# Feed forward part of a fused two-block kernel: eight raw slots in the second matrix product, another place for the residual loads and the additions, some sums of factors on GpSimd

## The chip, the cores and the metric

The kernel runs on one core of one Trainium2 chip. The metric is device time in microseconds of one execution, as the median over several runs. All work is in float32; a matrix product is made of three passes (see below), and the engines involved are TensorE (PE, with its weight loads PEld), VectorE (DVE), ScalarE (ACT), GpSimd (POOL) and SyncE, whose queue (SPq) issues every DMA of this kernel in one fixed order.

## The reference

Two model parts run one after the other: two layers of attention and mLSTM over 1024 tokens, and then a block of four mixers with an output projection, followed by the feed forward part that this change is in. The reference's feed forward, with `x` of 1024 tokens by 1024 channels:

```python
h = _rmsnorm(x, norm2_g)
u = h @ w_up            # 1024 x 4096
u = jnp.square(jax.nn.relu(u))
x = x + u @ w_down      # 4096 x 1024
return _rmsnorm(x, final_g)
```

## The kernel before

The feed forward is two large products, here called the up product (`up`, L2043) and the down product (`down`, L2105). Both use Strassen's scheme: each matrix is cut into 2x2 blocks, and seven products of sums of blocks (tables `UP` and `DOWN`) replace eight. For the down product a row of the table says which blocks of the hidden matrix are added or subtracted to make the left factor, which blocks of `w_down` make the right factor, and to which output blocks the result is added. Output block (t, n) is half t of the tokens and half n of the channels.

Each of the seven products is cut into eight units, j = 0 to 7. A unit is 24 matmuls of 128x128 by 128x512: every factor is split into a high and a low float32r half (`split`: a copy on ACT at L249 gives the high half, a subtraction on DVE at L250 gives the low half), and `mm3` (L244 to L246) multiplies high by high, high by low and low by high.

The data of a unit comes in as raw tiles of 128 x 1024 float32 (512 KB). In the up product these are weights only, one or two tiles per unit (L2034). In the down product they are weights (L2142) and those hidden blocks that were written to DRAM, tensor `hd` (L2134); the hidden blocks (1,0) and (1,1) stay on chip in 16 slots `H`. Per unit the seven down products load three, three, three, three, two, one and three raw tiles. All raw tiles go through one ring of six slots, two in the arena `fa` and four in the arena `t816a`; a load can only be issued when the slot's former owner has been read for the last time, that is after the sum (for the second tile of a sum) or after the low half at L250 (for the tile that holds the sum). When a factor is a sum of two blocks, DVE makes it (L2038 for up weights, L2022 for the left factors of the up product, L2119 in the down product).

The code makes the operands of a unit two units ahead of its matmuls. The results of a down product lie in four PSUM banks; the next product uses the other four. After each product DVE adds every bank to its output blocks in `x` (L2176, four or eight additions of 128x512). The rows of `x` in the first token half are complete after the fifth product, those of the second half after the seventh; then the final norm (`rms_row`: square on ACT at L469, three small steps on DVE and GpSimd, one scaling on DVE at L1382) and the store to `out` follow.

The order of the instructions on each engine is not the order of the code: the block is ordered by a scheduler that runs a timeline, and takes from each engine's waiting instructions by readiness and then by place in the code. Each engine then works through its own list in order, and an instruction that waits holds everything behind it on its engine.

Of the kernel before, what the change touches and what calls it, by code (L numbers as in the profile page):

```python
# [10 lines left out]
ALU = mybir.AluOpType  # L11
# [153 lines left out]
class Fill:  # L165
# [5 lines left out]
    def add(self, *gens):  # L171
        self.q.extend(gens)
# [9 lines left out]
    def finish(self):  # L182
        while self.q:
            self.step()
# [6 lines left out]
class Kernel:  # L191
# [1821 lines left out]
    def up_tokens(self, m):  # L2013

        blocks, op = self.UP[m][:2]
        h, l = self.rop.get([128, 4, 512]), self.rop.get([128, 4, 512])
        yield h, l
        for k in (0, 2):
            src = [self.z[:, 4 * c + k:4 * c + k + 2, t * 512:t * 512 + 512] for t, c in blocks]
            if op:  # L2020
                r = self.rtmp.get([128, 2, 512])
                self.nc.vector.tensor_tensor(r.ap, *src, op=op)  # L2022
                src = [r.ap]
            self.split(h[:, k:k + 2], l[:, k:k + 2], src[0])
            yield h, l

    def up_weights(self, m, j, raw):

        blocks, op = self.UP[m][2:4]
        rs = []  # L2030
        for k, n in blocks:
            r = raw.get([128, 4, 256])
            o = n * 2048 + j * 256
            self.nc.sync.dma_start(  # L2034
                r.ap, self.A["w_up_2"][0][k * 512:k * 512 + 512, o:o + 256].rearrange("(k p) c -> p k c", p=128))
            rs.append(r)
        if op:
            self.nc.vector.tensor_tensor(rs[0].ap, rs[0].ap, rs[1].ap, op=op)  # L2038
        h, l = self.rwh.get([128, 4, 256]), self.rwl.get([128, 4, 256])
        self.split(h.ap, l.ap, rs[0].ap)  # L2040
        return h, l

    def up(self, cur, raw, ahead):  # L2043

        nc, V = self.nc, self.nc.vector
# [10 lines left out]
        for i, (m, j) in enumerate(units):  # L2056
            if i + 2 < len(units):
                ahead.append(self.up_weights(*units[i + 2], raw))
            if j == 0:
                h, l = cur  # L2060
                nxt = self.up_tokens(m + 1) if m < 6 else None
            if nxt and j in (2, 3, 4):
                cur = next(nxt)
            w = ahead.pop(0)
            outs = [(c, sign, (c, j) not in acc) for c, sign in self.UP[m][4]]
            for c, _, first in outs:
# [38 lines left out]
    def down(self, raw):  # L2105
        nc, V, A = self.nc, self.nc.vector, self.A
        rw = Ring(self.xa, [4096 + 1024 * i for i in range(4)] + [1024 * i for i in range(4)], 1024)
        rx = self.F(0, 1024, 8)
        x = [rx.get() for t in range(8)]
        for t in range(8):  # L2110
            nc.sync.dma_start(x[t].ap, self.x4[t * 128:t * 128 + 128])
        fg = self.F(8192, 1024, 1).get()
        nc.sync.dma_start(fg.ap, A["final_g_2"].unsqueeze(0).broadcast_to([128, 1024]))
        self.rny = Ring(self.ta, [s[1] for s in self.cs.free_[:2]], 1024)

        def factor(rs, op, h, l):
            if op:
                r = rs[0][0] if rs[0][1] else rs[1][0] if rs[1][1] else raw.get([128, 2, 512])
                V.tensor_tensor(r.ap, rs[0][0].ap, rs[1][0].ap, op=op)  # L2119
            else:  # L2120
                r = rs[0][0]
            self.split(h.ap, l.ap, r.ap)

        def operands(m, j):
# [9 lines left out]
                    nc.sync.dma_start(r.ap, self.hd[f:f + 2].rearrange("f p t -> p f t"))  # L2134
                    rs.append((r, True))
            hid = self.rwh.get([128, 2, 512]), self.rwl.get([128, 2, 512])
            factor(rs, aop, *hid)
            rs = []
            for c, n in bb:
                r = raw.get([128, 2, 512])  # L2140
# [2 lines left out]
                    r.ap, A["w_down_2"][0][f:f + 256, n * 512:n * 512 + 512].rearrange("(f p) c -> p f c", p=128))  # L2143
                rs.append((r, True))
            w = rw.get([128, 2, 512]), rw.get([128, 2, 512])
            factor(rs, bop, *w)
            return hid, w

        def product(p, o, j, tt):
            (hh, hl), (wh, wl) = o  # L2150
            ts = slice(tt * 128, tt * 128 + 128)
            for i in range(2):
                self.mm3(p.ap, hh[:, i, ts], hl[:, i, ts], wh[:, i], wl[:, i], j + i == 0, j == 7 and i == 1)

        units = [(m, j) for m in range(7) for j in range(8)]
        ahead = [operands(*u) for u in units[:2]]
        todo = units[2:]
        for m in range(7):
            ps = [self.pg.get() for _ in range(4)]
            last = []  # L2160
            for j in range(8):
                if todo and not last:
                    ahead.append(operands(*todo.pop(0)))
                o = ahead.pop(0)
                if m == 6 and j >= 6:
                    last.append((j, o))
                    continue
                for tt in range(4):
                    product(ps[tt], o, j, tt)
                self.done([o[0]])  # L2170
            for tt in range(4):
                for j, o in last:
                    product(ps[tt], o, j, tt)
                for (t, n), sign in self.DOWN[m][4]:
                    y = x[4 * t + tt][:, n * 512:n * 512 + 512]
                    V.tensor_tensor(y, y, ps[tt].ap, op=ALU.add if sign > 0 else ALU.subtract)  # L2176
                if m in (4, 6):
                    t = 4 * (m == 6) + tt
                    self.rms_row(x[t].ap, fg.ap)
                    nc.sync.dma_start(A["out"][t * 128:t * 128 + 128], x[t].ap)  # L2180
        self.done([o[0] for _, o in last])

    def run(self):
# [49 lines left out]
```

## Time and profile before

| | |
|---|---|
| median of 3 runs | 2801.44 us (2795.85 to 2803.32) |
| profiled execution, its own time | 2799.03 us |
| its span, first to last instruction | 2797.3 us |
| PE busy | 2630.7 us (94%) |
| DVE busy | 1865.4 us (67%) |
| ACT busy | 1449.1 us (52%) |
| POOL busy | 481.5 us (17%) |
| mean granted TensorE clock | 0.979 of full speed |

The profiled execution is 2.4 us under the median of the runs. A matmul's record begins before the one in front of it has ended, so PE's busy time is not a measure of how full it is; the distance between the starts of matmuls is. The up product's matmuls begin at about 2141.0 us of the span, the down product's at about 2456.0, and the last matmul of all ends at 2789.4.

### The profile page before, as it was taken

The page shows a single profiled execution, that of the slowest core. Times are in us where ns is not written, and L with a number is a line of the kernel's source. Part 1 is how long each engine was busy: PE and PEld are TensorE (multiplying, and loading weights), DVE is VectorE, ACT ScalarE, POOL GpSimd, SP SyncE. Part 2 cuts the span into 40 slices and gives each one's busy share as a digit, 9 for nine tenths or more (in the row PEclk, how much of TensorE's full clock was granted, in tenths as well). Part 3 has the DMA queues.
Part 4 walks back from the last instruction along what each step waited for, and adds up shares of the span by engine and source line. Part 5 has one row for each costly group of instructions (what it writes and reads, how often), then busy time and mean ns, then how long its engine had stood idle before and what let it go on. Part 6 is the DMA issues. An engine that isn't in the chain of part 4 may idle for free. (4 is left out here: it accounts for less than half of the span.)

```text
span 2797.3 us, 43718 instructions
## 1 busy us (share of the span) xinstructions
PE 2630.7 (94%) x16222; PEld 2277.3 (81%) x16222; DVE 1865.4 (67%) x3750; ACT 1449.1 (52%) x3023; POOL 481.5 (17%) x686
## 2 busy tenths in 40 slices
PE   7999989999999999999998989898899999999998
PEld 3888878998889787978988878688798777877786
DVE  4788755536756788665365369977724586857886
ACT  4666545546624666555464153478715535643343
POOL 0122203414200122123132030144400000000000
PEclk9999999999999999999999989999899999999999
DMA  7001021212554101021124441422234667677855
GB/s 249 26 18 57 26 56 40 59 45 71 159 184 153 57 17 54 27 67 58 51 64 147 154 143 42 143 80 89 93 106 158 205 200 244 201 241 251 257 171 179
DMA packets 302241, 324.73 MB, mean 116 GB/s; under 512 B 17904, under 2 KB 242508, under 8 KB 301772
## 3 DMA queue, kind: packets, MB, share of 16 engines
q1 hardware_dynamic: 302028, 321.95, 36.5%
q8 instruction: 127, 2.08, 0.3%
q14 instruction: 86, 0.70, 0.1%
HBM read 274.86 MB, written 47.03 MB: 115 GB/s over the span
## 5 line engine op out<-in xcount | busy, mean ns | idle before, releaser
L246 PE MATMUL psum<-xa 128*128 128x512 f32 (+2 forms) x2136 | 751.4, 352 | 25.5 <-DVE xa L250 24.5
L244 PE MATMUL psum<-xa 128*128 128x512 f32 (+2 forms) x2136 | 757.5, 356 | 13.1 <-ACT xa L249 5.0
L245 PE MATMUL psum<-xa 128*128 128x512 f32 (+2 forms) x2136 | 751.2, 352 | 0.9 <-DVE xa L266 0.8
L246 PEld LDWEIGHTS psum<-xa 128*128 128x128 f32 x2136 | 408.8, 191 | 84.5 <-DVE xa L250 34.5
L244 PEld LDWEIGHTS psum<-xa 128*128 128x128 f32 x2136 | 409.9, 192 | 66.9 <-ACT xa L249 6.4
L245 PEld LDWEIGHTS psum<-xa 128*128 128x128 f32 x2136 | 409.1, 192 | 50.5 <-DVE xa L266 1.6
L464 POOL TENSOR_TENSOR rsb<-rsa,half 128x1 f32<-128x1 f32 (+1 forms) x129 | 93.9, 729 | 1088.1 <-DVE rsa L462 1017.1
L244 PE MATMUL psum<-xa,xg 128*128 128x256 f32 (+1 forms) x864 | 248.5, 288 | 1.9 <-DVE fa L1522 1.2
L245 PE MATMUL psum<-xa,xg 128*128 128x256 f32 (+1 forms) x864 | 246.1, 285 | 0.0
L246 PE MATMUL psum<-xa,xg 128*128 128x256 f32 (+1 forms) x864 | 245.8, 285 | 0.0
L249 ACT ACTIVATE xa<-t816a 128x1024 fp32r<-128x1024 f32 x125 | 131.0, 1056 | 206.6 <-DVE t816a L2119 110.9
L265 ACT ACTIVATE xa<-fa 128x1024 fp32r<-128x1024 f32 (+1 forms) x104 | 109.9, 1059 | 195.4 <-PE psum L246 110.5
L266 DVE TENSOR_TENSOR xa<-fa,xa 128x1024 fp32r<-128x1024 f32 (+1 forms) x94 | 115.3, 1229 | 133.6 <-ACT xa L265 123.1
L805 POOL TENSOR_SCALAR fa<-fa,esk 128x640 f32<-128x640 f32 (+2 forms) x144 | 112.1, 791 | 451.9 <-DVE esk L803 363.4
L244 PEld LDWEIGHTS psum<-xa,xg 128*128 128x128 f32 x864 | 164.0, 190 | 3.2 <-DVE fa L1522 1.6
L250 DVE TENSOR_TENSOR xa<-t816a,xa 128x1024 fp32r<-128x1024 f32 x125 | 151.3, 1219 | 21.2 <-ACT xa L249 13.1
L245 PEld LDWEIGHTS psum<-xa,xg 128*128 128x128 f32 x864 | 164.0, 190 | 0.8 <-issue 0.7
L246 PEld LDWEIGHTS psum<-xa,xg 128*128 128x128 f32 x864 | 163.7, 190 | 0.4 <-issue 0.3
L244 PE MATMUL psum<-xg,xa 128*128 128x512 f32 x376 | 153.2, 408 | 3.9 <-DVE fa L1764 2.8
L246 PE MATMUL psum<-xg,xa 128*128 128x512 f32 x376 | 151.7, 404 | 1.0 <-POOL xa L266 1.0
L245 PE MATMUL psum<-xg,xa 128*128 128x512 f32 x376 | 152.1, 404 | 0.2 <-DVE xg L250 0.2
L1008 DVE SCALAR_TENSOR_TENSOR fa<-fa,vec 128x640 f32<-128x640 f32 (+2 forms) x128 | 110.5, 869 | 51.7 <-ACT fa L1006 50.5
(500 smaller groups left out, 5870.4 us busy)
## 6 DMA issues: line engine op xcount, KB each, us to landing
fa<-in_w_in_dram SPq DMA_DIRECT2D x64, 512.0 KB
t816a<-in_w_up_dram SPq DMA_DIRECT2D x62, 512.0 KB
t816a<-in_w_down_dram SPq DMA_DIRECT2D x57, 512.0 KB
fa<-in_w_ada_dram SPq DMA_DIRECT2D x48, 512.0 KB
t816a<-hd SPq DMA_DIRECT2D x40, 512.0 KB
fa<-in_w_down_dram SPq DMA_DIRECT2D x39, 512.0 KB
fa<-in_w_up_dram SPq DMA_DIRECT2D x34, 512.0 KB
fa<-in_w_out_dram SPq DMA_DIRECT2D x24, 512.0 KB
```

The source lines that it names most:

```text
L244: mm(out, lh, rh, start=start, stop=False)
L245: mm(out, lh, rl, start=False, stop=False)
L246: mm(out, ll, rh, start=False, stop=stop)
L249: self.nc.scalar.activation(hi, src, AF.Copy)
L250: self.nc.vector.tensor_tensor(lo, src, hi.bitcast(F32), op=ALU.subtract)
L265: self.nc.scalar.activation(h.ap, r.ap, AF.Copy)
L266: (self.nc.gpsimd if self.wpool else self.nc.vector).tensor_tensor(l.ap, r.ap, h.ap.bitcast(F32), op=ALU.subtract)
L464: self.nc.gpsimd.tensor_tensor(r, e, self.half.broadcast_to([128, m]), op=ALU.pow)
L805: nc.gpsimd.tensor_scalar(P[j][:, :nk], P[j][:, :nk], e[:, j:j + 1], 0.0, op0=ALU.mult, op1=ALU.add)
L1008: nc.vector.scalar_tensor_tensor(y, U[i][:, lo + tap:hi + tap], col(tap), y, op0=ALU.mult, op1=ALU.add)
```

## The change

Five things change, in `up_tokens`, `up_weights`, `up` and `down`:

- In `down` the raw ring gets the two slots of the arena that are free by then, so it has eight; the two new ones are used first, and the scratch of the final norm moves to slots of hidden block (1,1).
- The loads of the residual `x` stand in `up` within the seventh product (L2069) and not at the head of `down` (L2111 before).
- In `down` the additions of a finished product are written one bank at a time between the units of the next product, and the final norm of the first token half is written within the seventh product, not after the fifth.
- In `down`, for products with a sum in both factors (the third, fourth and seventh), the left factor's sum of odd units goes to GpSimd: 12 sums.
- In `up`, the weight sum of odd units in the third product (4 sums) and both sums of the left factor of the fourth product (2 sums) go to GpSimd.

```diff
@@ up_tokens
-                self.nc.vector.tensor_tensor(r.ap, *src, op=op)
+                (self.nc.gpsimd if m == 3 else self.nc.vector).tensor_tensor(r.ap, *src, op=op)
@@ up_weights
-            self.nc.vector.tensor_tensor(rs[0].ap, rs[0].ap, rs[1].ap, op=op)
+            (self.nc.gpsimd if m == 2 and j % 2 else self.nc.vector).tensor_tensor(rs[0].ap, rs[0].ap, rs[1].ap, op=op)
@@ up
+            if m == 6:
+
+                if j == 0:
+                    rx, self.x = self.F(0, 1024, 8), []
+                self.x.append(rx.get())
+                nc.sync.dma_start(self.x[j].ap, self.x4[j * 128:j * 128 + 128])
@@ down
-        rx = self.F(0, 1024, 8)
-        x = [rx.get() for t in range(8)]
-        for t in range(8):
-            nc.sync.dma_start(x[t].ap, self.x4[t * 128:t * 128 + 128])
+        x = self.x
...
-        self.rny = Ring(self.ta, [s[1] for s in self.cs.free_[:2]], 1024)
-
-        def factor(rs, op, h, l):
+        o = raw.i % len(raw.slots)
+        raw.slots, raw.i = self.cs.free_ + raw.slots[o:] + raw.slots[:o], 0
+        self.rny = Ring(self.ta, [self.H[(1, 1), j].slot[1] for j in range(4)], 1024)
+
+        def factor(rs, op, h, l, eng):
             if op:
                 r = rs[0][0] if rs[0][1] else rs[1][0] if rs[1][1] else raw.get([128, 2, 512])
-                V.tensor_tensor(r.ap, rs[0][0].ap, rs[1][0].ap, op=op)
+                eng.tensor_tensor(r.ap, rs[0][0].ap, rs[1][0].ap, op=op)
...
-            factor(rs, aop, *hid)
+            factor(rs, aop, *hid, nc.gpsimd if bop and j % 2 else V)
...
-            factor(rs, bop, *w)
+            factor(rs, bop, *w, V)
...
+        def add(m, tt, p):
+            for (t, n), sign in self.DOWN[m][4]:
+                y = x[4 * t + tt][:, n * 512:n * 512 + 512]
+                V.tensor_tensor(y, y, p.ap, op=ALU.add if sign > 0 else ALU.subtract)
+
+        def finish(t):
+            self.rms_row(x[t].ap, fg.ap)
+            nc.sync.dma_start(A["out"][t * 128:t * 128 + 128], x[t].ap)
+
+        sums = []
         for m in range(7):
             ps = [self.pg.get() for _ in range(4)]
             last = []
             for j in range(8):
                 if todo and not last:
                     ahead.append(operands(*todo.pop(0)))
+                if sums:
+                    add(*sums.pop(0))
+                if m == 6 and 2 <= j < 6:
+                    finish(j - 2)
                 o = ahead.pop(0)
...
-            for tt in range(4):
-                for j, o in last:
-                    product(ps[tt], o, j, tt)
-                for (t, n), sign in self.DOWN[m][4]:
-                    y = x[4 * t + tt][:, n * 512:n * 512 + 512]
-                    V.tensor_tensor(y, y, ps[tt].ap, op=ALU.add if sign > 0 else ALU.subtract)
-                if m in (4, 6):
-                    t = 4 * (m == 6) + tt
-                    self.rms_row(x[t].ap, fg.ap)
-                    nc.sync.dma_start(A["out"][t * 128:t * 128 + 128], x[t].ap)
+            sums = [(m, tt, ps[tt]) for tt in range(4)]
+        for a in sums:
+            for j, o in last:
+                product(a[2], o, j, a[1])
+            add(*a)
+            finish(4 + a[1])
```

What the scheduler makes of it is seen in the lists of the engines. On DVE, at the passage from the first to the second down product, stood before (`psum` marks the additions; L250 is a low half into `xa`, L2119 a sum of two raw tiles):

```order
L250 TENSOR_TENSOR xa<-fa,xa 128x1024
L250 TENSOR_TENSOR xa<-t816a,xa 128x1024
L2176 TENSOR_TENSOR fa<-fa,psum 128x512 x2
L250 TENSOR_TENSOR xa<-t816a,xa 128x1024
L2119 TENSOR_TENSOR fa<-fa 128x1024
L2176 TENSOR_TENSOR fa<-fa,psum 128x512 x6
L250 TENSOR_TENSOR xa<-t816a,xa 128x1024
L250 TENSOR_TENSOR xa<-fa,xa 128x1024
```

And at the same place stands now (the additions are L2163, the sums L2124):

```order
L2124 TENSOR_TENSOR fa<-fa,t816a 128x1024
L250 TENSOR_TENSOR xa<-t816a,xa 128x1024
L2163 TENSOR_TENSOR fa<-fa,psum 128x512 x2
L250 TENSOR_TENSOR xa<-fa,xa 128x1024
L2163 TENSOR_TENSOR fa<-fa,psum 128x512 x5
L2124 TENSOR_TENSOR t816a<-t816a 128x1024
L2163 TENSOR_TENSOR fa<-fa,psum 128x512
L250 TENSOR_TENSOR xa<-fa,xa 128x1024
L250 TENSOR_TENSOR xa<-t816a,xa 128x1024 x2
```

The eight additions still stand together there, with one low half and one sum between them in both lists; counted over the whole list, 20 low halves of the down product stand before the first addition and 21 before the last, in both kernels. The sum that stood in front of six of the additions now stands in front of one.

On SyncE's list, at the end of the up product, stood before (`x4` is the residual, `hd` as the source is a hidden block coming back for the down product):

```order
L2111 DMA fa_70<-x4_80 128x1024 x2
L2034 DMA t816a_20302<-in_w_up_2_dram 128x4x256 x5
L2034 DMA fa_70<-in_w_up_2_dram 128x4x256
L2034 DMA t816a_20302<-in_w_up_2_dram 128x4x256
L2034 DMA fa_70<-in_w_up_2_dram 128x4x256
L2034 DMA t816a_20302<-in_w_up_2_dram 128x4x256 x2
L2034 DMA fa_70<-in_w_up_2_dram 128x4x256
L2034 DMA t816a_20302<-in_w_up_2_dram 128x4x256
L2034 DMA fa_70<-in_w_up_2_dram 128x4x256
L2034 DMA t816a_20302<-in_w_up_2_dram 128x4x256 x2
L2134 DMA t816a_20302<-hd_81 128x2x512 x2
```

And now (residual L2069, hidden blocks L2139):

```order
L2139 DMA t816a_20302<-hd_81 128x2x512
L2096 DMA hd_81<-t816a_20302 128x2x512
L2069 DMA fa_70<-x4_80 128x1024 x2
L2139 DMA t816a_20302<-hd_81 128x2x512
L2034 DMA t816a_20302<-in_w_up_2_dram 128x4x256 x3
L2139 DMA t816a_20302<-hd_81 128x2x512
L2034 DMA t816a_20302<-in_w_up_2_dram 128x4x256 x2
L2034 DMA fa_70<-in_w_up_2_dram 128x4x256
```

The residual loads stand at the same places among the weight loads and `hd` stores as before. Two loads of hidden blocks now stand ahead of the last 16 weight loads of the up product, and a third ahead of the last 13; before, the first such load had one weight load behind it.

GpSimd's list between the last norm in front of the feed forward and the final norm, as a difference (L464 is the power in the final norm, one element per partition):

```order
-L464 TENSOR_TENSOR rsb_23539<-rsa_23537,half 128x1
+L2038 TENSOR_TENSOR t816a<-t816a 128x1024 x2
+L2022 TENSOR_TENSOR t816a<-fa 128x1024
+L2038 TENSOR_TENSOR fa<-fa 128x1024
+L2022 TENSOR_TENSOR t816a<-fa 128x1024
+L2038 TENSOR_TENSOR fa<-fa 128x1024
+L2124 TENSOR_TENSOR t816a<-t816a 128x1024 x2
+L2124 TENSOR_TENSOR fa<-fa,t816a 128x1024
+L2124 TENSOR_TENSOR t816a<-t816a 128x1024 x3
+L2124 TENSOR_TENSOR fa<-fa,t816a 128x1024
+L2124 TENSOR_TENSOR t816a<-t816a 128x1024
+L464 TENSOR_TENSOR rsb_23872<-rsa_23870,half 128x1
```

Before, GpSimd had no work in this stretch.

## Rows read from the trace of the kernel before

**Rows 1.** Busy time per stretch: third up product, then down products 1, 2, 3, 4, 6, 7.

```profile
core 0: us, PE busy (x) PEld busy (x) DVE busy (x) ACT busy (x) POOL busy (x), PEclk, DMA share, GB/s
2228.28:2279.17 50.89, 46.05 (x194) 36.94 (x192) 41.28 (x51) 20.33 (x23) 0.00 (x0) 0.97 0.67 211
...
2455.99:2506.45 50.46, 45.05 (x194) 35.65 (x192) 29.20 (x28) 21.18 (x22) 0.00 (x0) 1.00 0.73 245
2506.45:2555.59 49.14, 45.75 (x194) 37.03 (x192) 36.49 (x36) 18.84 (x18) 0.00 (x0) 0.97 0.79 266
2555.59:2606.27 50.68, 46.76 (x193) 37.79 (x192) 42.13 (x41) 16.98 (x16) 0.00 (x0) 0.93 0.78 251
2606.27:2654.86 48.59, 45.47 (x194) 36.99 (x193) 41.10 (x40) 16.50 (x16) 0.00 (x0) 0.96 0.79 250
...
2698.86:2742.38 43.52, 43.52 (x194) 36.05 (x193) 34.27 (x37) 19.43 (x22) 6.71 (x4) 1.00 0.61 205
2742.38:2789.40 47.02, 44.88 (x193) 35.54 (x191) 37.30 (x40) 15.13 (x17) 1.51 (x3) 1.00 0.50 168
```

**Rows 2.** Waits in the down product: engine, line, releaser, us, times, longest.

```profile
PE psum L246 <- DVE xa L250: 17.2, 12, 3.6
```

**Rows 3.** The same for DVE, first and third down product alone.

```profile
DVE t816a L2119 <- DMA t816a<-hd: 15.6, 6, 5.7
...
DVE t816a L2119 <- DMA t816a<-hd: 7.3, 6, 2.2
```

**Rows 4.** The same for the SyncE queue, whole down product.

```profile
SPq L2142 <- DVE xa L250: 84.7, 51, 10.0
SPq L2134 <- DVE xa L250: 64.4, 38, 5.4
```

**Rows 5.** Timeline where the second down product begins: start, us, instruction, idle before it.

```profile
2515.63 1.22 DVE L2119 TENSOR_TENSOR fa<-fa 128x1024 f32<-128x1024 f32 x1 [2.17 <-DMA fa<-in_w_down_dram]
2516.77 3.67 DVE L2176 TENSOR_TENSOR fa<-fa,psum 128x512 f32<-128x512 f32 x6
...
2520.36 1.22 DVE L250 TENSOR_TENSOR xa<-t816a,xa 128x1024 fp32r<-128x1024 f32 x1
2521.50 1.22 DVE L250 TENSOR_TENSOR xa<-fa,xa 128x1024 fp32r<-128x1024 f32 x1
...
2521.63 0.50 PE L246 MATMUL psum<-xa 128*128 128x512 f32 x1 [3.06 <-DVE xa L250]
```

**Rows 6.** GpSimd, a sum of this size, by shape: busy us, mean ns.

```profile
L1934 POOL TENSOR_TENSOR t604a<-t604a 128x1024 f32<-128x1024 f32 x12 | 28.9, 2412 | 27.5 <-ACT t604a L1933 27.5
```

**Rows 7.** Timeline, GpSimd and DVE together, in an earlier stage.

```profile
1610.27 0.43 DVE L1290 TENSOR_TENSOR fa<-fa 128x256 f32<-128x256 f32 x1
...
1610.92 2.40 POOL L1354 TENSOR_TENSOR t604a<-fa 128x1024 f32<-128x1024 f32 x1 [102.92 <-DVE fa L1290]
1611.07 2.53 DVE L1290 TENSOR_TENSOR fa<-fa 128x256 f32<-128x256 f32 x1
```

**Rows 8.** Timeline, another place, GpSimd's instruction begun under a DVE one.

```profile
1810.76 1.28 DVE L1936 SCALAR_TENSOR_TENSOR t604a<-t604a,drs 128x1024 f32<-128x1024 f32 x1
...
1811.01 3.26 POOL L266 TENSOR_TENSOR xa<-fa,xa 128x1024 fp32r<-128x1024 f32 x1 [28.36 <-ACT xa L265]
...
1811.95 1.22 DVE L1920 CUSTOM_DVE_ANT_0 t604a<-psum,fa 128x1024 f32<-128x1024 f32 x1
```

**Rows 9.** GpSimd's power in the final norm: by shape, and three during DVE work.

```profile
L464 POOL TENSOR_TENSOR rsb<-rsa,half 128x1 f32<-128x1 f32 x116 | 77.7, 670 | 1021.2 <-DVE rsa L462 964.6 <-DVE den L1183 22.2 <-DVE AB L438 16.9
...
2705.30 6.17 POOL L464 TENSOR_TENSOR rsb<-rsa,half 128x1 f32<-128x1 f32 x3 [3.58 <-DVE rsa L462]
```

**Rows 10.** Timeline in the third up product, unit j = 1: weight sum, low half, matmul.

```profile
2234.56 1.23 DVE L2038 TENSOR_TENSOR t816a<-t816a 128x1024 f32<-128x1024 f32 x1 [4.49 <-DMA t816a<-in_w_up_dram]
2235.70 1.22 DVE L250 TENSOR_TENSOR xa<-t816a,xa 128x1024 fp32r<-128x1024 f32 x1
...
2236.97 0.50 PE L246 MATMUL psum<-xa 128*128 128x512 f32 x1 [2.29 <-DVE xa L250]
```

## Prediction

> **What bounds the kernel now.** I read the busy time by product first, then the waits of PE, then those of DVE and of the SyncE queue, and last the timeline at the places where PE stands. In the stretches by product [rows 1] the reader is to compare each length with that of the sixth down product, 43.52 us for 192 matmuls without a stall: that is PE's pace, 5.44 us for a unit of 24 matmuls, and no product can be shorter. The first four down products took 50.46, 49.14, 50.68 and 48.59 us, so they lost 6.9, 5.6, 7.2 and 5.1 us, 24.8 in all; the seventh lost 3.5 and the third up product 7.4. More than these 35.7 us the change cannot win, and most of it is in the down product.
>
> PE itself waits there for the low half of a factor on DVE, 12 times, 17.2 us [rows 2]. The rest of the loss is the granted clock: in the second, third and fourth product its mean is 0.97, 0.93 and 0.96 [rows 1], because after a stall such as the 3.06 us one [rows 5] the engine runs for a while at 1.2 GHz, not 2.4; a mean of 0.97 over 49.14 us is some 3 us at half speed. A stall avoided brings that back too.
>
> DVE is late because it waits for raw tiles: 15.6 us for hidden blocks in the first product, still 7.3 in the third [rows 3]. The tiles are late because SyncE cannot issue their loads before a low half has freed a slot: 84.7 and 64.4 us of its waiting [rows 4]. So the circle is slot, load, sum, low half, slot. In the third and fourth product DVE is also nearly full by itself. Two low halves that follow each other start 1.14 us apart (2520.36, 2521.50), and six additions take 3.67 us, 0.60 each [rows 5]. Eight units of two sums and two low halves and eight additions are 32 x 1.14 + 8 x 0.60 = 41.3 us, against PE's 43.5.
>
> **Eight slots.** The first down product is the clean case: 50.46 us for 8 units is 6.31 us per unit, and six slots hold two units of three tiles, so a slot went round in 12.6 us. Eight slots hold 2.67 units; with the same round a unit could come every 4.7 us, faster than PE needs it. The round will not stay the same, since more loads are in flight: if it grows as the traffic has to (from 50.46 to 43.5 us for the same bytes, by 16%) it is 14.7 us, or 5.5 us per unit, 44 us for the product. The DMA share would go from 0.73 to 0.85 [rows 1], which leaves room. The ends are 43.5 and the present 50.46; I take 45, with a little for the start: -5.5. The second product has the same three tiles per unit and one sum, and its loss is around one place: a sum 2.17 us late for a weight load, six additions behind it, then the low half that PE wants [rows 5]. Two more slots let loads go out two thirds of a unit, 3.6 us, earlier, which covers the 2.17 us and the 3.06 us stall. Ends 43.5 and 49.1; I take 44.5: -4.6.
>
> **Additions one by one.** The list of DVE hardly changed: the eight additions stand together still, between the same low halves. I cost this at 0 (one sum of 1.14 us passes five additions and could be early or late by as much, so +-1 us). The residual loads stand where they stood: 0. The final norm of the first half stands at the same place as well: 0; from the last matmul to the end of the span, 2789.4 to 2797.3, nothing changes.
>
> **Sums on GpSimd.** This is the part that can go wrong. A sum of 128x1024 takes GpSimd 2.41 us [rows 6] where DVE gives up 1.14. And the two do not run beside each other: a DVE sum that takes 0.43 us alone took 2.53 when it was begun 0.15 us after a GpSimd sum, and ended after that had ended [rows 7]. The other way round, GpSimd took 3.26 us when a DVE instruction with two SBUF inputs was ahead of it; the DVE instruction behind, which reads PSUM, kept its 1.22 [rows 8]. Low halves and sums read SBUF twice; the additions read PSUM once. So a sum moved to GpSimd takes 1.14 us from DVE and locks its low halves and sums for up to 2.4. With all of it in a row the third and fourth product need 28 x 1.14 + 8 x 0.60 + 4 x 2.41 = 46.4 us of DVE; where GpSimd falls into DVE's own waits or beside the additions, less, down to 37, and PE's 43.5 decides. The Trainium skill ("GPSIMD Engine Reference", Engine selection) would keep an elementwise sum on VectorE because GpSimd is about twice as slow for two inputs, and its Key points name the contention with VectorE instructions that have two SBUF inputs. The first rule alone would leave DVE at 37 us and these products at 43.5, 5 us better in sum than I forecast; by the second, as in the rows, they stand near 46.4.
>
> I take 46 for each, since with 41.3 us of other work per product there is little DVE waiting left to hide in: -4.7 and -2.6. The ends are 43.5 and what they are now. The seventh product has the same sums, with the norm of the first half before it and without a lead to lose: +0.5, between -3.5 and +3. In the up product, PE waits at unit j = 1 of the third product for a weight sum, 4.49 us late for its DMA, and the low half after it [rows 10]; this sum is now on GpSimd and ends at least 2.41 - 1.14 = 1.3 us later, and the ring there still has six slots. DVE gains there, as its additions from PSUM can run beside GpSimd. I take +1.2; the ends are -2, where the relief of DVE wins, and +5.1, where all four sums delay PE by 1.3.
>
> Behind a late GpSimd sum stand the copy on ACT and then the low half, which DVE waits for in order; every later sum, low half and addition is queued behind that wait, and with them the slots that SyncE waits for.
>
> **Sum.** -5.5 - 4.6 - 4.7 - 2.6 + 0.5 + 1.2 = -15.7 us, made against the profiled execution's 2799.03 us (span 2797.3): 2783.3. The median of the runs lies 2.4 us above that execution, so 2786 us, 0.6% faster.
>
> **Rivals.** (1) GpSimd eats the gain. The first two products gain their 10.1, the third and fourth stay as long as they are (46.4 us of DVE plus the DMA waits that remain), the seventh loses 3 and the up product 5.1: -2.0, about 2799. For it speaks that DVE was at 41.3 of 43.5 already; against it, that 46.4 is still below 50.7 and 48.6. (2) The other side, slower: GpSimd is starved. Three of its powers, 0.67 us each as a rule, took 6.17 us while DVE worked through low halves and sums [rows 9]. That is 4.2 us late, 1.4 each. If a moved sum waits like that, it ends 1.3 + 1.4 = 2.7 us later than on DVE. With the 4 of the up product's third and the 8 of the down product's third and fourth all on PE's path, that is 32 us, less the 10.1 us that the first two products gain and the 12.3 that the third and fourth would no longer lose in their old way: about +10, 2811. It decides as soon as odd units, and only those, are what PE waits for; the units made ahead (10.9 us of lead) speak against it. (3) The DMA engines are the bound and not the slots: shares of 0.73 to 0.79 are means over stretches with stalls. Then a load just takes longer, the products stay, and the up product's 1.2 remains: 2803. Against it speaks the sixth product's rate of 205 GB/s at 0.61, which scales to over 330 at a full share, while 24 tiles in 43.5 us are 289. (4) All of it works and GpSimd is hidden: -24.8 and -3.5, 2773.
>
> **How the numbers follow.** My forecast 2776 to 2794 gets 0.58, rival 4 0.06, rival 1 0.15, rival 3 0.08, rival 2 0.13. A difference of under 0.3% (8.4 us) cannot be told from none here. Faster: the forecast nearly whole and rival 4, 0.63. Same: rivals 1 and 3, less a little that falls outside, 0.22. Slower: rival 2 and that little, 0.15. The range runs from rival 4's 2773 to 2805, which takes in rivals 1 and 3 and leaves rival 2 out.
>
> **What would show it.** Right: the first two down products at 44 to 46 us with the clock at 1.00; SyncE's waits for L250 down by a third or more; third and fourth near 46; DVE instructions of 2 to 3.5 us beside GpSimd's sums in L2124. Wrong: the first product still near 50 (slots were not it); PE's stalls on odd units only (rival 2); the third up product above 55; additions spread out in the trace and a gain at the passages between products that the lists don't explain.

## The result and the profile after

The changed kernel took 2814.36 us (median of 9 runs, 2804.10 to 2823.17), the kernel before 2795.85 us beside it (9 runs, 2789.61 to 2803.32). The ratio is 1.0061, interval 1.0047 to 1.0075: slower by 0.6%, some 17 us. A second comparison (below) gave 1.0057 [1.0041, 1.0072]. The forecast was 2786 us, range 2773 to 2805: wrong in sign. The profiled execution of after took 2823.17 us, the longest of its nine; its up product began at 2145.7 us of the span, 4.7 us later than before, where the code is the same. So part of what its profile shows is this one execution.

The busy time by product again, as in [rows 1] and with the same columns: third up product, then down products 1, 2, 3, 4, 6, 7.

```profile
core 0: us, PE busy (x) PEld busy (x) DVE busy (x) ACT busy (x) POOL busy (x), PEclk, DMA share, GB/s
2233.59:2289.13 55.54, 48.99 (x194) 38.89 (x192) 42.61 (x47) 20.72 (x23) 12.27 (x5) 0.91 0.63 202
2469.87:2514.10 44.23, 43.86 (x193) 35.97 (x192) 24.57 (x23) 19.75 (x20) 0.00 (x0) 1.00 0.72 242
2514.10:2574.37 60.27, 51.17 (x194) 40.03 (x192) 38.31 (x37) 17.82 (x18) 3.44 (x2) 0.89 0.68 221
2574.37:2625.19 50.82, 46.52 (x193) 37.94 (x192) 43.44 (x36) 14.31 (x15) 9.76 (x4) 0.93 0.73 244
2625.19:2676.81 51.62, 46.33 (x193) 37.59 (x192) 43.04 (x37) 19.14 (x19) 8.13 (x3) 0.93 0.77 256
2720.33:2763.85 43.52, 43.52 (x193) 36.05 (x192) 36.32 (x35) 18.36 (x21) 12.15 (x6) 1.00 0.63 218
2763.85:2813.58 49.73, 46.71 (x193) 37.73 (x191) 38.32 (x38) 15.62 (x18) 7.59 (x5) 0.93 0.40 137
```

The first product is as forecast, 50.46 to 44.23. The second is not: 49.14 before, 44.5 forecast, 60.27 now, and no GpSimd sum of its own is in it. The third stayed, the fourth and seventh grew by 3.0 and 2.7, the third up product by 4.7. PE's waits for low halves in the down product, as in [rows 2], are fewer and longer (8 for 12, 22.0 us for 17.2). SyncE's waits for L250, which were to fall by a third, did not fall: 152.8 us for the 149.1 of [rows 4].

```profile
PE psum L246 <- DVE xa L250: 22.0, 8, 5.3
...
SPq L2147 <- DVE xa L250: 101.9, 56, 13.6
SPq L2139 <- DVE xa L250: 50.9, 32, 3.8
```

**Where the second product went.** [rows 4] shows SyncE's waits for low halves alone. Before, it also waited 90 us for sums, the two largest parts of it below, and little for another weight tile to land (whole down product; engine, line, releaser, us, times, longest):

```profile
SPq L2142 <- DVE t816a L2119: 56.8, 26, 6.1
SPq L2142 <- DVE fa L2119: 22.8, 14, 4.0
...
SPq L2142 <- DMA fa<-in_w_down_dram: 5.8, 2, 4.2
```

In the second product of after the wait for a weight tile to land is its largest; before, it had none there:

```profile
SPq L2147 <- DMA t816a<-in_w_down_dram: 20.0, 6, 4.9
```

And DVE waits there for weights (23.4 us of such waits for 12.2 before; the largest part):

```profile
DVE t816a L2124 <- DMA t816a<-in_w_down_dram: 15.6, 5, 5.3
```

The timeline of SyncE's queue and of DVE in that stretch shows how the two waits belong together (start, us, instruction, idle before it):

```profile
2507.43 1.50 SPq L2147 DMA_DIRECT2D t816a<-in_w_down_dram  x2
2509.85 0.37 SPq L2139 DMA_DIRECT2D t816a<-hd  x1
2516.24 1.50 SPq L2147 DMA_DIRECT2D t816a<-in_w_down_dram  x2
2518.65 0.37 SPq L2139 DMA_DIRECT2D t816a<-hd  x1
2523.85 1.50 SPq L2147 DMA_DIRECT2D t816a<-in_w_down_dram  x2
2527.31 0.37 SPq L2139 DMA_DIRECT2D fa<-hd  x1
2531.84 0.37 SPq L2147 DMA_DIRECT2D t816a<-in_w_down_dram  x1
```

```profile
2514.99 1.23 DVE L2124 TENSOR_TENSOR t816a<-t816a 128x1024 f32<-128x1024 f32 x1 [5.17 <-DMA t816a<-in_w_down_dram]
2516.13 2.49 DVE L250 TENSOR_TENSOR xa<-t816a,xa 128x1024 fp32r<-128x1024 f32 x2
2522.59 1.23 DVE L2124 TENSOR_TENSOR fa<-fa,t816a 128x1024 f32<-128x1024 f32 x1 [3.97 <-DMA t816a<-in_w_down_dram]
...
2530.59 1.23 DVE L2124 TENSOR_TENSOR t816a<-t816a 128x1024 f32<-128x1024 f32 x1 [0.31 <-DMA t816a<-in_w_down_dram]
```

The sums here are those of units 1, 2 and 3. After each of them weight loads go out 1.25 us after the sum begins, which is when it ends (2514.99 and 2516.24, 2522.59 and 2523.85, 2530.59 and 2531.84). The next sum then waits for the second load of the pair, which is issued 1.1 us after the first and lands some 5 us later. Eight slots, and one unit under way: 7.6 and 8.0 us from sum to sum where PE needs a unit in 5.44. Read from the engines' lists, the slots and waits of the five loads issued from 2507.43 on are:

| load on SyncE | slot had | waits for |
|---|---|---|
| first weight tile, j = 3 | second weight tile, j = 0 | sum of j = 0 |
| second weight tile, j = 1 | hidden block two units back | low half behind the sum of j = 0 |
| hidden block, j = 3 | first weight tile, j = 0 | low half after that |
| first weight tile, j = 4 | second weight tile, j = 1 | sum of j = 1 |
| second weight tile, j = 2 | hidden block, j = 0 | low half behind the sum of j = 1 |

With three tiles per unit going round eight slots, a second tile no longer follows a second tile. It follows a hidden block, and is issued behind the sum of the unit before it. The sum of unit 1 waits for a load that waited for the sum of unit 0. With six slots a second tile takes the slot of the second tile two units back, freed by that unit's sum, and two units are under way. That is theory S: the order in which the slots go round costs the second product its time. The rivals are G (the ring helps, GpSimd's sums lose) and D (more loads share the DMA engines and each lands later).

**What GpSimd's sums do.** GpSimd and DVE in the fourth product, where PE stood 5.29 us at unit j = 2:

```profile
2638.92 2.55 POOL L2124 TENSOR_TENSOR fa<-fa,t816a 128x1024 f32<-128x1024 f32 x1 [11.19 <-DMA fa<-hd]
```

```profile
2635.66 2.47 DVE L2163 TENSOR_TENSOR fa<-fa,psum 128x512 f32<-128x512 f32 x4
2638.05 1.22 DVE L2124 TENSOR_TENSOR t816a<-t816a 128x1024 f32<-128x1024 f32 x1
2639.18 3.37 DVE L250 TENSOR_TENSOR xa<-fa,xa 128x1024 fp32r<-128x1024 f32 x1
```

```profile
2642.61 0.80 PE L246 MATMUL psum<-xa 128*128 128x512 f32 x1 [5.29 <-DVE xa L250]
```

The low half begun 0.26 us after a GpSimd sum took 3.37 us, not 1.22, and ended after it: the lock of [rows 7], at the low half that PE waits for. The first matmul after the stall takes 0.80 us where a full clock gives 0.39 to 0.50, and the product's mean clock is 0.93. The same happened at unit j = 2 of the third, fourth and seventh product in all three profiles of kernels with the circle and all twelve sums (the changed kernel twice, no up sums): in all nine that low half took 3.36 to 3.39 us, and PE stood 4.3 to 5.3 us in the third and fourth product, 3.0 to 3.7 in the seventh. In the third up product the same happens to the low half at j = 2, beside a sum of the next product's left factor (L2022), not beside the weight sum of [rows 10]:

```profile
2245.75 2.35 POOL L2022 TENSOR_TENSOR t816a<-fa 128x1024 f32<-128x1024 f32 x1 [2.64 <-DVE t816a L2038]
```

```profile
2246.19 3.00 DVE L250 TENSOR_TENSOR xa<-fa,xa 128x1024 fp32r<-128x1024 f32 x1
```

GpSimd itself is not slow. Nine of its twelve sums of the down product took 2.74 us on average, and none of the twelve more than 3.20, near [rows 6] and [rows 8]:

```profile
L2124 POOL TENSOR_TENSOR t816a<-t816a 128x1024 f32<-128x1024 f32 x9 | 24.7, 2743 | 384.1 <-DMA t816a<-hd 384.1
```

### The profile page after: what moved, and what is told of

The parts are those of the page before. It is cut to its first block, busy times and chain, and to the rows that moved or that the text cites. A ratio compares the mean times of both kernels' runs of the same rounds, so it can differ in the third digit from the quotient of the medians.

```text
span 2821.4 us, 43725 instructions
## 1 busy us (share of the span) xinstructions
PE 2647.5 (94%) x16222; PEld 2291.3 (81%) x16222; DVE 1871.4 (66%) x3732; ACT 1444.7 (51%) x3023; POOL 527.0 (19%) x704
## 5 line engine op out<-in xcount | busy, mean ns | idle before, releaser
L246 PEld LDWEIGHTS psum<-xa 128*128 128x128 f32 x2136 | 414.4, 194 | 92.7 <-DVE xa L250 41.8
L244 PEld LDWEIGHTS psum<-xa 128*128 128x128 f32 x2136 | 414.6, 194 | 69.0 <-ACT xa L249 5.7
L245 PEld LDWEIGHTS psum<-xa 128*128 128x128 f32 x2136 | 414.2, 194 | 51.1 <-issue 1.0
L250 DVE TENSOR_TENSOR xa<-t816a,xa 128x1024 fp32r<-128x1024 f32 x127 | 167.1, 1329 | 38.7 <-ACT xa L249 28.5
L464 POOL TENSOR_TENSOR rsb<-rsa,half 128x1 f32<-128x1 f32 (+1 forms) x129 | 94.2, 731 | 526.6 <-DVE rsa L462 455.6
```

What stands on the lines that cost most here:

```text
L244: mm(out, lh, rh, start=start, stop=False)
L245: mm(out, lh, rl, start=False, stop=False)
L246: mm(out, ll, rh, start=False, stop=stop)
L250: self.nc.vector.tensor_tensor(lo, src, hi.bitcast(F32), op=ALU.subtract)
L464: self.nc.gpsimd.tensor_tensor(r, e, self.half.broadcast_to([128, m]), op=ALU.pow)
```

## The experiments

Ratios are to the kernel before, timed beside each; a profile is one execution, so single lengths carry some chance. A circle is one ring whose slots are taken in turn; by use means three rings, with three slots for left tiles, three for right ones and two for the second tile of a sum.

| kernel | slots in down | sums on GpSimd | ratio | interval |
|---|---|---|---|---|
| changed kernel, again | circle of 8 | 18 | 1.0057 | 1.0041 to 1.0072 |
| no up sums | circle of 8 | 12, down | 1.0052 | 1.0039 to 1.0065 |
| without j = 5 | circle of 8 | 15 | 1.0029 | 1.0014 to 1.0044 |
| only j = 5 | circle of 8 | 9 | 1.0018 | 1.0005 to 1.0030 |
| no down sums | circle of 8 | 6, up | 1.0015 | 1.0003 to 1.0028 |
| no sums | circle of 8 | 0 | 1.0003 | 0.9989 to 1.0017 |
| ring only | circle of 8 | 0 | 1.0002 | 0.9988 to 1.0016 |
| weights first | circle of 8 | 0 | 1.0016 | 1.0003 to 1.0028 |
| GpSimd only | circle of 6 | 18 | 1.0019 | 1.0005 to 1.0033 |
| by use | 3 + 3 + 2 | 18 | 1.0006 | 0.9990 to 1.0021 |
| by use, no sums | 3 + 3 + 2 | 0 | 0.9996 | 0.9984 to 1.0009 |
| circle, then by use | both | 0 | 0.9987 | 0.9976 to 0.9999 |

**Ring only.** The kernel before, with

```diff
...
+        o = raw.i % len(raw.slots)
+        raw.slots, raw.i = self.cs.free_ + raw.slots[o:] + raw.slots[:o], 0
-        self.rny = Ring(self.ta, [s[1] for s in self.cs.free_[:2]], 1024)
+        self.rny = Ring(self.ta, [self.H[(1, 1), j].slot[1] for j in range(2)], 1024)
```

> The kernel before with the eight-slot ring alone (norm scratch in two dead slots); no sum on GpSimd, additions and residual loads as before. Theory S (the rotation of eight slots over three tiles a unit makes the load of a second weight tile wait for a low half that stands behind the sum of the unit before, so one second tile is under way at a time; 7.5 us a unit): first down product 44 to 46 us, second 57 to 62, up product as before, 1 to 8 us slower in all. Theory G (the ring helps, the sums on GpSimd lose): first and second 44 to 46, all 8 to 15 us faster. Theory D (more loads under way share the DMA engines, each lands later): second above 55, and so it is in every kernel with eight slots.

1.0002. First product 44.60, second 51.80, third 52.62, seventh 43.68; the up product as before. S in kind (what the first product gains, the second and third lose), but the second was 5 us shorter than S said, and the whole was not 1 us slower. G's 8 us of gain are not there: the interval reaches 0.12%, 3.4 us.

**No sums on GpSimd.** The changed kernel with `V` for `nc.gpsimd` at all three places.

> The changed kernel with all 18 moved sums back on VectorE. S: second down product still 57 to 62, third up product back to 50 to 52, fourth and seventh down product back to 48.6 and 47 or better; within 8 us of the kernel before. G: second 44 to 46, 8 to 15 us faster than before. If the additions' new place in the code is the cause of the second product's loss, it is slow here and not in the ring-only kernel.

1.0003; second product 58.55, third 46.91, fourth 48.41, seventh 43.68. So the second product's loss does not need GpSimd, and the additions and residual loads cost nothing that can be told from the ring alone, 1.0002 (each figure is uncertain by 0.14%, 4 us). Within the second product the additions may matter all the same. In the ring alone and in weights first (below), DVE's list has six additions in front of the sum of unit 3, and the second product took 51.8 and 53.0 us; in the seven others with the circle there, that sum stands in front of the sixth addition, and it took 54.7 to 60.3. No run changes this place alone.

**Slots by use.** The changed kernel with the eight slots in three rings:

```diff
...
-        raw.slots, raw.i = self.cs.free_ + raw.slots[o:] + raw.slots[:o], 0
+        s = self.cs.free_ + raw.slots[o:] + raw.slots[:o]
+        raws = [Ring(self.ta, [], 1024) for _ in range(3)]
+        for r, k in zip(raws, ((0, 3, 6), (2, 5, 7), (1, 4))):
+            r.slots = [s[i] for i in k]
+        left, right, second = raws
...
-                    r = raw.get([128, 2, 512])
+                    r = (second if rs and rs[0][1] else left).get([128, 2, 512])
...
-                r = raw.get([128, 2, 512])
+                r = (second if rs else right).get([128, 2, 512])
...
```

> The changed kernel with its eight slots given out by use instead of in one circle: three for the left tile that holds a sum, three for the right one, two for the second tile of a sum; GpSimd's sums stay. S: each second tile takes the slot of the second tile two units back, so two are under way; second down product 44 to 47 us, 10 to 16 us faster than the changed kernel, near the kernel before (within 8 us). D: second still above 55, since as many loads can be under way. G: no more than 3 us better than the changed kernel.

1.0006. Second product 48.36: D falls, with the same slots and a higher DMA share (0.81). SyncE's wait for weight tiles is gone there. But it stayed above the 44 to 47 us that S said, and the first product is back at 48.89; that two slots for second tiles are too few there is my reading, not tested by itself.

**GpSimd only.** The kernel before with the 18 sums moved and six slots.

> The kernel before with the 18 sums on GpSimd alone, six slots. S gives GpSimd's sums the rest of the loss: third up product 54 to 56, the up product 6 to 10 us longer, third, fourth and seventh down products 0 to 3 us longer each, second unchanged at 49, 8 to 16 us slower in all. G: the same places, 15 to 25 us slower and the second down product longer as well. The forecast's sizes: up +1.2, third and fourth near 46 or unchanged, no more than 5 us either way.

1.0019, 5 us: less than S or G said, and at the edge of what the forecast's sizes allow. The third up product was 48.97, not longer. So GpSimd's price is not a fixed one; it is larger with the circle of eight. In this kernel, and with slots by use, where 18 sums cost some 0.1%, the low half before PE's stall at j = 2 of the third and fourth product took 1.2 to 1.5 us, not 3.4, and the seventh product had no stall over 0.8 us.

**The changed kernel again.** No edit.

> The changed kernel itself once more, beside the next three: its ratio should be near 1.006 again. Its profile is a second execution. If the 60.3 us second down product and the 55.5 us third up product belong to the kernel, they are 57 to 62 and 54 to 56 again; if they were one execution's chance, the second down product is 49 to 54 as in the ring-only kernel and the third up product 49 to 51 as with GpSimd's sums alone.

1.0057. Its second profile, with the columns of the first (down products 2, 3, 4, 7):

```profile
2517.18:2572.24 55.06, 46.47 (x193) 36.81 (x192) 34.76 (x35) 15.50 (x16) 2.39 (x1) 0.97 0.72 229
2572.24:2625.14 52.90, 46.60 (x194) 37.70 (x193) 44.13 (x37) 16.19 (x17) 10.51 (x5) 0.94 0.75 245
2625.14:2676.52 51.38, 46.14 (x194) 37.63 (x193) 41.86 (x36) 18.31 (x19) 7.96 (x3) 0.93 0.79 250
...
2763.98:2812.74 48.76, 44.66 (x193) 35.71 (x191) 38.89 (x38) 15.62 (x18) 7.94 (x5) 1.00 0.42 142
```

The second product was neither of the two expected cases but at 55.06 between them, with 8.6 us of PE's stalls where the first profile had 9.0; the rest of the difference is the clock, 0.97 for 0.89. The third up product was 52.94.

**By use, no sums.** Both edits.

> The changed kernel with slots given out by use and all 18 sums on VectorE. S: the second product has no circle (46 to 49) and GpSimd's price is gone: 4 to 12 us faster than before, a ratio of 0.996 to 0.9985. If GpSimd's sums cost nothing where the slots don't tie the loads together, it is the same as the by-use kernel with them, 1.000. If additions and slots matter only through the passage from up to down product, first product 48 to 50 and the whole 0 to 4 us slower than before.

0.9996, 1 us: S's smallest gain, 0.9985, is at the edge of the interval. First product 48.87, as in the last case, second 48.26, as by S.

**No up sums, no down sums.** `V` for `nc.gpsimd` in `up_weights` and `up_tokens`, or in `down`.

> The changed kernel with the six sums of the up product back on VectorE; the twelve of the down product stay on GpSimd. If the up product's sums carry the loss (9 us of the profile's 20): 1.002 to 1.003, third up product 50 to 51. If the down product's sums carry it, by holding VectorE's list in the third, fourth and seventh product while the circle of eight slots waits: 1.005 to 1.006.

> The changed kernel with the twelve sums of the down product back on VectorE; the six of the up product stay on GpSimd. The other half of the run before: if the up product's sums carry the loss, 1.003 to 1.006 with the third up product at 54 to 56; if the down product's do, 1.000 to 1.002, third and fourth down product 47 to 49.

1.0052 and 1.0015: the twelve sums of the down product carry the loss, 0.42% or 12 us between the changed kernel and the one without them. Without them the third, fourth and seventh product took 48.58, 48.50 and 43.68. The up product's six cost 0.05 to 0.12%, 1 to 3 us, which is within the noise of these differences (some 0.2%).

**Without j = 5, only j = 5.** `nc.gpsimd if bop and j in (1, 3, 7)`, or `j == 5`.

> The changed kernel with the sums of unit j = 5 in the third, fourth and seventh down product (3 of the 18) back on VectorE. In both profiles of the changed kernel just this sum runs on GpSimd while VectorE makes the low half that TensorE waits for at unit j = 2, right after the additions; that low half takes 3.4 us, not 1.2. Theory L (the lock counts only where it meets that low half): stalls at j = 2 of 5.3, 5.2 and 3.4 us fall to about 3, 3 and 1; third, fourth and seventh down product 47 to 50, 47 to 50 and 44 to 46; ratio 1.002 to 1.003. Theory A (every sum on GpSimd costs alike, about 1 us): ratio 1.005.

> The changed kernel with only the sums of unit j = 5 of the down product on GpSimd, the other nine back on VectorE; the six of the up product stay. L: the stalls at j = 2 stay near 5 us in the third and fourth product, ratio 1.004 to 1.005. A: a quarter of the down sums' price, ratio 1.002 to 1.003.

Without j = 5: 1.0029, as L said; A's 1.005 lies outside. The low half at the same place of the fourth product took 1.21 us and PE's stall 3.13:

```profile
2634.74 1.21 DVE L2124 TENSOR_TENSOR t816a<-t816a 128x1024 f32<-128x1024 f32 x1
2635.88 1.21 DVE L250 TENSOR_TENSOR xa<-fa,xa 128x1024 fp32r<-128x1024 f32 x1
```

```profile
2637.14 0.80 PE L246 MATMUL psum<-xa 128*128 128x512 f32 x1 [3.13 <-DVE xa L250]
```

Only j = 5: 1.0018, where L said 1.004 to 1.005. L's lock is not refuted by that; the sums did not fall where L expected them:

```profile
2578.76 6.17 POOL L2124 TENSOR_TENSOR fa<-fa,t816a 128x1024 f32<-128x1024 f32 x1 [308.12 <-DMA fa<-hd]
2630.22 3.27 POOL L2124 TENSOR_TENSOR fa<-fa,t816a 128x1024 f32<-128x1024 f32 x1 [45.28 <-DMA fa<-hd]
2761.16 3.24 POOL L2124 TENSOR_TENSOR fa<-t816a,fa 128x1024 f32<-128x1024 f32 x1 [39.25 <-DMA fa<-hd]
```

In none of the three products did the sum hold up the low half that PE wanted. In the fourth it began 0.19 us after that low half, which kept 1.22 us; the next one was held up, to 3.40 us (4.54 for two), but PE did not wait for it:

```profile
2630.03 1.22 DVE L250 TENSOR_TENSOR xa<-fa,xa 128x1024 fp32r<-128x1024 f32 x1
2631.17 4.54 DVE L250 TENSOR_TENSOR xa<-t816a,xa 128x1024 fp32r<-128x1024 f32 x2
```

```profile
2631.31 0.79 PE L246 MATMUL psum<-xa 128*128 128x512 f32 x1 [4.33 <-DVE xa L250]
```

So the 4.3 us of this stall are not the lock's. In the third product the sum was begun during a DVE sum, took 6.17 us itself, and three low halves behind that DVE sum kept 1.22 us each; the stalls there were 1.57 and 0.92. In the seventh the longest stall was 0.62. What a sum costs depends on where it meets DVE's list: 3 sums alone cost 0.03%, 9 alone 0.14%, all 12 0.42% (differences to the kernel without down sums, each uncertain by some 0.2%). The 12 cost more than the 3; that they cost more than the 3 and the 9 together (0.25%) is not clear of that noise. What moves the sum of j = 5 onto the low half when all twelve are there is open.

**Weights first.** In the code of a unit, the hidden blocks behind the weight tiles; no sums on GpSimd.

> Eight slots in one circle, no sum on GpSimd, and in the code of a unit the weight tiles stand before the hidden blocks, so that a second weight tile takes the slot of the hidden block three units back, not two. S read from the lists: SyncE's list still has the first tile of unit u + 3 (waiting for the sum of u) in front of the second tile of u + 1, and that waits for a low half behind the same sum on VectorE; one unit under way, second down product 52 to 60 us again, ratio 1.000 to 1.002. If only the distance of the slot counted: 44 to 49, 5 to 10 us faster than before.

1.0016; second product 52.95, and 50.27 in the seventh up product, which was not expected. The slot's distance alone did not help, as S said from the lists; SyncE still waited 18.4 us there for weight tiles to land.

**Circle, then by use.** The slots by use, and in the places of `left`, `right`, `second` still `raw` (the circle) where `m` is 0; no sums on GpSimd.

> No sum on GpSimd; the eight slots go round in one circle in the first down product and are given out by use from the second on. S: first product 44 to 46 as with the circle, second to fourth 46 to 50 as by use, seventh 43.7; ratio 0.997 to 0.999, the best of the kernels here. If the first product's gain is only borrowed and paid back in the second, second above 52 and the ratio 1.000.

0.9987 [0.9976, 0.9999], 2799.52 us against 2802.56: the lowest ratio here (not clear of by use, no sums, 0.9996), and as expected in each product. Down products 1 to 4 and 7:

```profile
2466.31:2510.88 44.57, 43.82 (x194) 35.98 (x193) 28.20 (x27) 20.47 (x21) 0.00 (x0) 1.00 0.76 247
2510.88:2559.46 48.58, 45.94 (x193) 36.97 (x192) 37.11 (x37) 18.62 (x19) 0.00 (x0) 0.96 0.81 277
2559.46:2608.08 48.62, 45.44 (x194) 37.18 (x193) 41.96 (x41) 16.41 (x16) 0.00 (x0) 0.96 0.79 259
2608.08:2654.68 46.60, 43.83 (x193) 35.98 (x192) 43.68 (x43) 16.77 (x16) 0.00 (x0) 1.00 0.73 239
...
2741.72:2785.40 43.68, 43.68 (x193) 35.87 (x191) 32.26 (x36) 14.57 (x17) 1.55 (x3) 1.00 0.36 121
```

The first product keeps the circle's gain and the second does not pay it back. SyncE's wait for a weight tile in the second product is 1.8 us, once, where after had 20.0:

```profile
SPq L2152 <- DMA t816a<-in_w_down_dram: 1.8, 1, 1.8
```

## Why the prediction was wrong

The first step that failed is "Eight slots", and in it the second product: "Two more slots let loads go out two thirds of a unit, 3.6 us, earlier". It took eight slots for a depth. In a circle, which slot a tile gets decides what it waits for, and eight slots with three tiles per unit put a second weight tile behind the sum of the unit before. In the nine profiles with the circle there, the second product took 51.8 to 60.3 us, mean 56.3; in the three with slots by use 48.3 to 48.6, in the two with six slots 49.1 and 46.3. The reading "SyncE cannot issue their loads before a low half has freed a slot" left out a large part of it: the 90 us that SyncE waited for sums, which free the second tiles. Nor did the slots by use bring the 44.5 that was forecast: in all three of those profiles PE still stood 2.45 to 2.80 us at j = 2, behind the additions, so this stall is not one of the slots alone. The first product, 45 forecast, took 43.7 to 45.8 with the circle in all ten profiles. There two hidden blocks and one weight tile make a unit and the sum is one of hidden blocks, and the argument of the slot's round held.

The second is "Sums on GpSimd", 46 us for the third and fourth product each. DVE's time came out inside the bounds given, 37 to 46.4 us: after has 43.44 and 43.04. The step that failed is from there to the product's length: it took DVE's total for the limit. But DVE's time is not short on the whole; it is short at unit j = 2, behind the additions. There PE stood 3.57 and 3.12 us before, and still 3.11 and 2.43 in the changed kernel without down sums, so the 46 was missed without any lock too: in the six kernels with eight slots and no down sum on GpSimd the third product took 46.9 to 52.6 us and the fourth 46.6 to 48.5. A lock at that place goes straight into PE's stall (5.3 and 5.2 us in the second profile). The seventh was put at +0.5 from the same total; by the ring it fell to 43.68, and by the locks it rose to 48.8 and 49.7.

By the ratios, the ring alone, which was to win the first two products' 10.1 us, lost 0.02%, under 1 us. The products with moved sums (third, fourth, seventh and the up product) were to win 5.6 us together; moving the sums cost 0.54% (1.0057 less 1.0003), some 15 us.

By size: first product 44.1 for 45 (mean of the two profiles of after), second 57.7 for 44.5, third 51.9 for 46, fourth 51.5 for 46, seventh 49.2 for 47.5, third up product 54.2 for 52.1. These differences sum to 27.5 us. The two profiled executions lie 39 us above the forecast's 2783.3; the other 12 us stand at places that it put at nothing, 5 of them in front of the up product, where the code is the same, and the rest in the other up products. The median missed the forecast by 28 us. That the 27.5 comes so near it is luck: the two profiled executions lie 9 and 3 us above their medians, and the kernel before was 5.6 us faster in this comparison than the median that the forecast started from.

The up product's term of +1.2 was of the right size, 1 to 3 us by the ratios, but not for its reason. It had PE wait longer at unit j = 1. That wait, 1.8 to 2.5 us in the seven profiles without its sums on GpSimd, is under 0.8 in the seven with them; in these the low half at j = 2 is held up instead, to 3.0 us in every one, and PE stands 2.7 to 3.4 us there. The third up product took 49.0 to 55.5 us in the seven with its sums on GpSimd and 50.4 to 53.8 in the seven without, no difference. The fourth took 44.4 to 47.7 with and 43.5 in every one without; its sums of the left factor were not costed.

Rival 2 gave 2811 us, close to the measured time by luck, and is not what happened. GpSimd was not starved: its sums took 2.4 to 3.2 us in after, and the one of 6.17 us seen above cost little. In the down products with moved sums PE's stalls of over 2 us all stand at j = 2, an even unit, where rival 2 wanted the odd ones. The lock went the other way, GpSimd holding DVE. The Trainium skill ("SBUF — State Buffer", SBUF: two separate sides) says that a VectorE instruction with two SBUF inputs and a GpSimd one that reads SBUF exclude each other for the whole of the one that started first. The 3.37 us low half agrees: GpSimd's sum ended at 2641.47, the low half 1.08 us later. The sum of 6.17 us agrees only in part: it began under one VectorE sum, but ended 2.26 us behind the third of the low halves that followed, so a row of VectorE instructions kept it out, not the first alone. The forecast had this row's like in [rows 7] and used it as a load on DVE, not as a delay.

Rival 3 (the DMA engines as the bound, so the products stay) fell in the first product, which went to 44 us at a share of 0.72 to 0.76. The others were not at their bound either: with slots by use the second ran at 0.81 and 271 GB/s, for 0.79 and 266 before. Rival 1 (GpSimd eats the gain of the first two products) is half true: the twelve sums cost 12 us, but there was no gain to eat, since the ring alone gave 1.0002. Additions and residual loads were put at 0, and 1.0003 beside 1.0002 bears that out within their intervals. The tail stayed: 7.8 us from the last matmul to the end, 7.9 before.

What stays open: how much of the second product's spread of 8 us, with the same list of loads there in all but weights first, comes from the place of the sixth addition and how much from chance; why the stall at j = 2 stays with slots by use; and how much of the down sums' 12 us is the lock itself and how much the clock that falls after some of the stalls.

## What to carry to other kernels

A ring of slots is not only a depth: write down, for one round, which tile had each slot and which instruction frees it, and see whether any load waits behind work that needs the load before it. When tiles of a unit are freed by different instructions, a ring that is a multiple of the unit keeps like behind like (the six slots here), and slots by use do the same for other numbers; neither was best for every product here, so look at each product's list. Work moved to GpSimd is paid where it meets the VectorE instruction that TensorE waits for, so cost it at that place and not in VectorE's total.

## What the runs showed of the hardware

After stalls of about the same length the clock did not always fall. After 3.02 us in the seventh product (first profile) the matmuls took 0.79, then 0.63 us, 1.2 GHz; after 3.38 us at the same place of the second profile, 0.50, then 0.40, and the product's clock was 1.00:

```profile
2778.37 0.79 PE L246 MATMUL psum<-xa 128*128 128x512 f32 x1 [3.02 <-DVE xa L250]
2778.96 0.63 PE L244 MATMUL psum<-xa 128*128 128x512 f32 x1
```

```profile
2778.86 0.50 PE L246 MATMUL psum<-xa 128*128 128x512 f32 x1 [3.38 <-DVE xa L250]
2779.20 0.40 PE L244 MATMUL psum<-xa 128*128 128x512 f32 x1
```

In the first profile 3.2 us stand on top of that stall (49.73 - 43.52 - 3.02), with a mean clock of 0.93. In the second it is 1.9 us (48.76 - 43.52 - 3.38) at a clock of 1.00, with another wait of 0.63 among them. So the same stall can bring some us of slow clock or none, and two executions of one kernel can differ by that.
